# Squares summed by a stationary block of ones in column quarters, z tiles made half a group ahead, y kept in the place of X, and the rope tables made inside the first feed-forward stage

## The chip, the cores and the metric

One Trainium2 chip, of which the kernel uses 1 core. The metric is the device time of one execution in microseconds (us). The kernel before the change took 1360.01 us (median of 3 runs, 1358.56 to 1360.58). One more execution was recorded by the hardware profiler: it took 1358.62 us, of which the profile's span covers 1356.9.

Engines are named as in the profile: PE is TensorE (matrix multiplication), PEld its loading of weights, DVE is VectorE, ACT is ScalarE, POOL is GpSimd, SP is SyncE, which here issues the DMAs. Banks are the eight PSUM tiles `ps` of 128 x 512 that PE writes.

## What is computed

A decoder trunk of 512 tokens by 1024 channels in float32: one Mamba-2 (SSD) layer, a feed-forward layer, one multi-head latent attention layer (MLA), a second feed-forward layer, each with a post-normalisation. The change lies in the SSD layer and in the rotary tables that MLA reads:

```python
zxbcdt = x @ in_proj                       # z, x, B, C and dt side by side
xbc = silu(causal_depthwise_conv(xbc, conv_w, conv_b))
dt = softplus(dt + dt_bias);  A = -exp(A_log)
# 8 groups of 4 heads of 64 channels, state 128; 4 chunks of 128 tokens:
cum = cumsum(dt * A);  decay = exp(where(causal, cum[t] - cum[s], -inf))
w = einsum(C, B) * decay * dt
y = einsum(w, x) + einsum(C, state) * exp(cum)
state = state * exp(cum[-1]) + einsum(exp(cum[-1] - cum) * dt, x, B)
y = (y + D * x) * silu(z)                  # 256 channels a group
y = y * rsqrt(mean(y * y over the group) + 1e-5) * norm_g
h = y @ out_proj                           # then the norm, feed-forward, MLA, feed-forward
cos, sin = cos(positions * inv_freq), sin(positions * inv_freq)   # 512 x 32
```

## The kernel before, in words

Channels lie on partitions and tokens along the free axis. Every large product is taken in three passes over a high and a low part: weights come by DMA on SP into one of three buffers `wst`, ACT casts them to `wh` (L60), DVE takes the rest `wl` (L61), and six such pairs are kept, split up to four items ahead (five in the first feed-forward). `WStream` hands them out in the order of a list of items. `bulk` (matmuls at L123) turns one item of 128 output channels into one bank: 24 matmuls with 512 moving columns.

**The SSD stage** (0 to about 433 us of the span) goes through 8 groups. For each group the program writes four conv tiles, B, C, X0 and X1 (`a_tile`: a bulk, then ACT scales the bank at L438, DVE adds three taps at L440, ACT takes a tanh at L442, DVE finishes at L443), then two z tiles (`z_tiles`: a bulk, then a tanh on ACT at L506 and L507 on DVE). Group 0 has its z from the front of the kernel, where PE computes it beside dt.

The scan of a group is a chain of six steps:

- s0 loads the group's cumulated decays into W by DMA.
- s1 multiplies C with B (L525) and transposes B (L528); DVE masks the result (L530), ACT makes CE (L537), which POOL multiplies by C (L538), and turns W into the decay by 16 relus (L542) and one exponential over 2048 columns (L543).
- s2 transposes X on PE (L550); DVE multiplies W by the masked product (L554) and makes xdt (L559) and wx (L561).
- s3 multiplies wx with B to new states (L568; ACT and DVE chain them at L570 to L575) and W with xdt (L579).
- s4 adds the states' part (L587), then makes y: L593 adds D * x, L594 multiplies by z, ACT squares (L595) and scales by the norm's weight into `yT` (L598), DVE takes its low part (L599), and L602 adds the two squares to `sq` (128 channels by 512 tokens).
- s5 sums `sq` over its 128 partitions: four matmuls at L608 with `sq` as the stationary operand and one moving column of ones; DVE (L610) and POOL (L611) make `rstd`.

The steps stand in a list with due times (`later`). After each tile a clock made by hand advances by its expected time (`tick`), and a step is written into the program once its condition holds, with lags between the steps from `LAG`. Between the tiles of most groups stand blocks of the output projection (`out_block`, matmuls at L129 to L131, added to `h` by DVE at L149). On PE, ACT, DVE and POOL a scheduler then sets the final order from the program's dependences, with its own estimates; each engine runs its own instructions strictly in the order so fixed. On SP the order is that of the program.

The buffers matter: `one` holds a single buffer for each name, so W, CE, bk, xdt, wx (which shares its place with `sq`), y and the pair of z tiles `zs` are each there once; conv tiles have eight buffers. The residual x goes into `h` by one DMA in group 1 (L726), and ACT scales it in group 2 (L729).

**The first feed-forward** (`ffn`, from about 433 us) goes through its 22 hidden tiles with two products each, in two rounds. Between SSD and `ffn` the program builds the rotary tables (`rope_tables`): two small DMAs on SP, some ten small DVE instructions, one sine on ACT.

The order of the work after that point is the same in both kernels on every engine.

Of the kernel before, what the change touches and what calls it, by code (L numbers as in the profile page):

```python
# [9 lines left out]
F32 = mybir.dt.float32  # L10
# [8 lines left out]
P = 128  # L19
# [227 lines left out]
    nc.vector.tensor_tensor(gt[:, 1, :], av, gt[:, 0, :], op=ALU.subtract)  # L247


def ffn(k, ws, base, cwp, gb, la=2, out=None):  # L250

    nc, tc = k.nc, k.tc
    with ExitStack() as c:
# [7 lines left out]
        for r in range(2):  # L261
            gts = []
            def finish(ci, bg, bv):
                gt = pools["gt"].tile([P, 2, SEQ], F32R, name="gt")
                conv3_silu_gate(k, pools, bg, bv, cw, ci, gt)
                gts.append(gt)
# [18 lines left out]
            for ci in range(c0, r * 11 + 11):  # L285
                bg, bv = k.bank(), k.bank()
                ws.ahead(n + 1)
                for b, i in ((bg, n), (bv, n + 1)):
                    w = [x.rearrange("p (k m) -> p k m", k=KT) for x in ws.get(i)]
                    k.mm_a(b, w, k.ht, slice(0, 512))  # L290
                    ws.retire(i)
                n += 2
                ws.ahead(n)
                finish(ci, bg, bv)
            for hf in range(2):
                sl = slice(hf * 512, (hf + 1) * 512)
                final = r == 1 and hf == 1
# [63 lines left out]
def ssd_items(xbc, zdt, zw, ow):  # L361

    it = []
    for a, b in ZDT:
        it.append((zdt[:, a:b, :], (b - a) * ZW))
    for g in range(NG):
        for t in (16 + g, 24 + g, 2 * g, 2 * g + 1):
            it.append((xbc[t], 1024))
        for j in range(2 if g else 0):
            it.append((zw[2 * g + j], 1024))  # L370
        if g in OUT_AT:
            it += [(ow[r * P:(r + 1) * P, :], 1024) for r in (2 * OUT_AT[g], 2 * OUT_AT[g] + 1)]
    it += [(ow[r * P:(r + 1) * P, :], 1024) for r in range(2 * NG - 6, 2 * NG)]
    return it


def ssd(k, ws, base, xT, x, cwp, hv, ngp, gb):
    nc, tc = k.nc, k.tc
    with ExitStack() as cx:
# [129 lines left out]
        def chain(g):  # L509
# [73 lines left out]
            def s4():  # L583
                yb = S["yb"]
                for c in range(1, NT):
                    for t, e, h in heads:
                        nc.tensor.matmul(yb[t][e * HD:(e + 1) * HD, c * P:(c + 1) * P], S["st"][c - 1][:, h * HD:(h + 1) * HD],  # L587
                                         S["CE"][:, h, (c - 1) * P:c * P], start=False, stop=True, skip_group_check=True)
                q = [thp.tile([P, SEQ], F32, name="th") for _ in range(2)]
                y = one.tile([P, 2, SEQ], F32, name="y")  # L590
                for t in range(2):
                    j = 2 * g + t
                    nc.vector.scalar_tensor_tensor(y[:, t], S["X"][t], ng[:, 1, j:j + 1], yb[t], op0=ALU.mult, op1=ALU.add)  # L593
                    nc.vector.scalar_tensor_tensor(y[:, t], y[:, t], 0.5, S["z"][:, t], op0=ALU.mult, op1=ALU.mult)  # L594
                    nc.scalar.activation(q[t], y[:, t], AF.Square)  # L595
                    yt = ytp.tile([P, 2, SEQ], F32R, name="yT")
                    sc = ng[:, 0, j:j + 1]
                    nc.scalar.activation(yt[:, 0, :], y[:, t], AF.Copy, scale=sc)  # L598
                    nc.vector.scalar_tensor_tensor(yt[:, 1, :], y[:, t], sc, yt[:, 0, :], op0=ALU.mult, op1=ALU.subtract)  # L599
                    S.setdefault("yT", []).append(yt)  # L600
                S["sq"] = one.tile([P, SEQ], F32, name="sq", tag="wx")
                nc.vector.tensor_tensor(S["sq"], q[0], q[1], op=ALU.add)  # L602

            def s5():

                b = k.bank()
                for c in range(NT):
                    nc.tensor.matmul(b[:, c:c + 1], S["sq"][:, c * P:(c + 1) * P], ones[:, 0:1], start=True, stop=True)  # L608
# [4 lines left out]
            S.update(s0=s0, s1=s1, s2=s2, s3=s3, s4=s4, s5=s5)  # L613

        T = [0.0]
        todo = []
# [20 lines left out]
            G[g]["s0"]()  # L637
            ran["w", g] = T[0]

        def z_tiles(g):  # L640
            S = G[g]
            S["z"] = one.tile([P, 2, SEQ], F32, name="zs")
            for t in range(2):
                z_gate(S["z"][:, t], bulk())
                tick(5.2)

        def z_turn():

            zs = G[0]["z"] = one.tile([P, 2, SEQ], F32, name="zs")
            for t in range(2):  # L650
                b = k.bank()
                for c in range(NT):
                    nc.tensor.transpose(b[:, c * P:(c + 1) * P], D["z0"][:, c, t * P:(t + 1) * P], k.ident)
                nc.scalar.copy(zs[:, t], b)
# [65 lines left out]
        for g in range(NG):  # L720
            S = G[g]
            if g == 0:
                z_dt()
            S["B"] = a_tile(16 + g)
            if g == 1:
                nc.sync.dma_start(k.h, x.rearrange("(i p) d -> p i d", p=P))  # L726
            if g == 2:
                for i in range(NT):
                    nc.scalar.mul(k.h[:, i, :], k.h[:, i, :], ALPHA)  # L729
# [448 lines left out]
```

## Time and profile before

| | value |
|---|---|
| runs | 1360.01 us median, 1358.56 to 1360.58 |
| profiled execution | 1358.62 us, span 1356.9 |
| granted TensorE clock, mean | 0.998 |
| PE busy | 1341.7 us (99%) |
| DVE busy | 885.6 us (65%) |
| ACT busy | 585.6 us (43%) |
| POOL busy | 71.5 us (5%) |
| SSD stage on PE | 0 to 433.1 us |

How to read the views that follow. The *page* gives busy times by engine and the shares of the chain of waits, which is followed back from the last instruction. *Waits* has, for each engine and line, what ended its idle time: total us, number of times, the longest. The *timeline* has one row for each burst of instructions: start and length in us, engine, line and operation, output and inputs with their shapes, how many instructions, and in brackets the idle time ahead of it with what ended it. The *chain of waits* lists start, length and piece. Line numbers are those of the kernel before; in the changed kernel the steps from s1 to s4 stand one line further down.

### The profile page before, as it was taken

The numbers are of one execution on the slowest core, as the hardware profiler recorded it, in microseconds if no ns is written. First come the engines' busy times: TensorE is split into PE (matmuls) and PEld (weight loads), VectorE is DVE, ScalarE is ACT, GpSimd is POOL, SyncE is SP. The second block draws the span as 40 slices with busy tenths as digits, with TensorE's granted clock in tenths as the row PEclk, the third lists the DMA queues.
The fourth block names the chain that finished last, engine by engine and source line by source line (L and its number), as shares of the span: only waits on it lengthen the run. The fifth ranks groups of instructions, "written<-read, shape, count | busy, mean of one in ns | idle before, by whom it ended". The sixth has DMA issues, their size and how long they took to land.

```text
span 1356.9 us, 17211 instructions
## 1 busy us (share of the span) xinstructions
PE 1341.7 (99%) x6819; PEld 1127.2 (83%) x6819; DVE 885.6 (65%) x1355; ACT 585.6 (43%) x927; POOL 71.5 (5%) x73
## 2 busy tenths in 40 slices
PE   9999999999999999999999999999999999999997
PEld 8878888888888888888888889888898888888886
DVE  7888778778788765425565366998576553465534
ACT  5765536526523544323443134665254431344421
POOL 0111101001102000000000021000100000000001
PEclk9999999999999999999999999999999999999999
DMA  7432332323232433232322222211052322323211
GB/s 240 179 118 95 108 120 82 109 100 103 96 106 64 143 102 100 85 101 95 106 95 85 85 88 65 92 48 63 31 189 93 98 96 89 106 94 102 91 55 63
DMA packets 44433, 135.14 MB, mean 100 GB/s; under 512 B 4768, under 2 KB 5792, under 8 KB 42816
## 3 DMA queue, kind: packets, MB, share of 16 engines
q1 hardware_dynamic: 44352, 134.04, 30.2%
q8 instruction: 53, 0.87, 0.3%
q14 instruction: 28, 0.23, 0.1%
HBM read 131.86 MB, written 2.16 MB: 99 GB/s over the span
## 4 chain that ended last, share of the span: by engine, by line
PE 91%; DVE 5%; DMA 2%; ACT 1%; issue 1%; POOL 0%; SPq 0%; POOLq 0%; DVEq 0%; ACTq 0%
PE ps L123 54%; PE ps L129 9%; PE ps L130 9%; PE ps L131 9%; PE ps L996 2%; PE ps L579 1%; PE ps L1031 1%; DVE wl L61 1%; PE ps L587 1%; PE ps L568 1%; DMA wst<-in_hw_dram 1%; PE ps L1018 1%; PE ps L680 1%; PE ps L205 1%; PE ps L525 0%
## 5 line engine op out<-in xcount | busy, mean ns | idle before, releaser
L123 PE MATMUL ps<-ht,wh 128*128 128x512 f32 (+1 forms) x2272 | 520.2, 379 | 0.8 <-ACT ht L208 0.8
L123 PEld LDWEIGHTS ps<-ht,wh 128*128 128x128 f32 x2272 | 408.4, 188 | 79.8 <-issue 1.2
L61 DVE TENSOR_TENSOR wl<-wst,wh 128x1024 fp32r<-128x1024 f32 (+3 forms) x226 | 273.9, 1217 | 155.9 <-ACT wh L60 155.6
L60 ACT CAST wh<-wst 128x1024 fp32r<-128x1024 f32 (+3 forms) x226 | 228.0, 1014 | 225.7 <-PE ps L131 171.0
L123 PE MATMUL ps<-ht,wl 128*128 128x512 f32 (+1 forms) x1136 | 267.2, 377 | 0.0
L123 PEld LDWEIGHTS ps<-ht,wl 128*128 128x128 f32 x1136 | 205.8, 188 | 39.5
L130 PE MATMUL ps<-wl,gt 128*128 128x512 f32 (+1 forms) x363 | 140.5, 387 | 0.0
L129 PE MATMUL ps<-wh,gt 128*128 128x512 f32 (+1 forms) x363 | 140.1, 386 | 0.0
L131 PE MATMUL ps<-wh,gt 128*128 128x512 f32 (+1 forms) x363 | 138.6, 382 | 0.0
L240 DVE SCALAR_TENSOR_TENSOR acc<-ps,cw,acc 128x511 f32<-128x511 f32 x88 | 65.5, 747 | 99.5 <-ACT acc L239 99.5
L440 DVE SCALAR_TENSOR_TENSOR cv<-ps,cw,cv 128x511 f32<-128x511 f32 (+2 forms) x96 | 71.5, 746 | 28.6 <-ACT cv L438 27.9
L239 ACT ACTIVATE acc<-ps,cw 128x512 f32<-128x512 f32 x88 | 68.4, 778 | 40.2 <-PE ps L123 40.2
L129 PEld LDWEIGHTS ps<-wh,gt 128*128 128x128 f32 x363 | 68.1, 188 | 14.9
L131 PEld LDWEIGHTS ps<-wh,gt 128*128 128x128 f32 x363 | 68.1, 188 | 14.4
L130 PEld LDWEIGHTS ps<-wl,gt 128*128 128x128 f32 x363 | 68.3, 188 | 12.8
L246 ACT CAST gt<-acc 128x512 fp32r<-128x512 f32 x44 | 27.3, 621 | 98.9 <-DVE acc L245 98.9
L149 DVE SCALAR_TENSOR_TENSOR h<-h,ps 128x512 f32<-128x512 f32 x47 | 31.2, 684 | 56.7 <-PE ps L131 56.7
L241 DVE SCALAR_TENSOR_TENSOR acc<-ps,cw,acc 128x510 f32<-128x510 f32 x88 | 65.7, 748 | 2.8
L244 ACT ACTIVATE acc<-acc 128x512 f32<-128x512 f32 x44 | 27.8, 632 | 87.0 <-DVE acc L241 86.9
L149 DVE SCALAR_TENSOR_TENSOR h<-ps,rstd,h 128x512 f32<-128x512 f32 x64 | 46.3, 749 | 21.9 <-PE ps L131 21.3
L159 POOL TENSOR_SCALAR lnst<-lnst 128x1 f32<-128x1 f32 x15 | 11.9, 796 | 870.7 <-ACT lnjunk L158 870.7
L129 PE MATMUL ps<-wh,yT 128*128 128x512 f32 x128 | 51.8, 405 | 0.0
(227 smaller groups left out, 1549.8 us busy)
## 6 DMA issues: line engine op xcount, KB each, us to landing
wst<-in_up_dram SPq DMA_DIRECT2D x88, 512.0 KB, 3.4
wst<-in_down_dram SPq DMA_DIRECT2D x40, 512.0 KB, 3.6
wst<-in_xbc_dram SPq DMA_DIRECT2D x32, 512.0 KB, 3.7
W<-cumd SPq DMA_DIRECT2D x8, 1024.0 KB, 4.6
wst<-in_sow_dram SPq DMA_DIRECT2D x16, 512.0 KB, 3.6
wst<-in_zw_dram SPq DMA_DIRECT2D x14, 512.0 KB, 3.5
lngb<-in_gb_dram SPq DMA_DIRECT2D x4, 1024.0 KB, 6.0
wst<-in_aow_dram SPq DMA_DIRECT2D x8, 512.0 KB, 3.4
```

Source lines behind the costliest of these rows:

```text
L60: nc.scalar.copy(h[:, :f], s[:, :f])
L61: nc.vector.tensor_tensor(l[:, :f], s[:, :f], h[:, :f], op=ALU.subtract)
L123: nc.tensor.matmul(out, w[:, k, :], xts[k][:, x, ts], start=first and p == 0 and k == 0, stop=last and p == 2 and k == nk - 1, skip_group_ ...
L129: nc.tensor.matmul(out, xt[:, 0, tsl], wh, start=start, stop=False, skip_group_check=True)
L130: nc.tensor.matmul(out, xt[:, 0, tsl], wl, start=False, stop=False, skip_group_check=True)
L131: nc.tensor.matmul(out, xt[:, 1, tsl], wh, start=False, stop=stop, skip_group_check=True)
L149: self.nc.vector.scalar_tensor_tensor(hs, a, scale, b, op0=ALU.mult, op1=ALU.add, **kw)
L239: nc.scalar.activation(a, b, AF.Identity, bias=cw[:, ch, 3:4], scale=cw[:, ch, 2:3])
L240: nc.vector.scalar_tensor_tensor(a[:, 1:], b[:, :SEQ - 1], cw[:, ch, 1:2], a[:, 1:], op0=ALU.mult, op1=ALU.add)
L241: nc.vector.scalar_tensor_tensor(a[:, 2:], b[:, :SEQ - 2], cw[:, ch, 0:1], a[:, 2:], op0=ALU.mult, op1=ALU.add)
L244: nc.scalar.activation(ag, ag, AF.Silu)
L440: nc.vector.scalar_tensor_tensor(t[:, d:], b[:, :SEQ - d], cw[:, ch, 3 - d:4 - d], t[:, d:], op0=ALU.mult, op1=ALU.add)
```

## The change

It has four parts.

1. **The sum of squares.** Where s5 had `sq` as the stationary operand and one column of ones moving, it now has 32 columns of ones stationary and a chunk of 128 tokens of `sq` moving. Each of the four matmuls writes 32 equal rows, chunk c to the rows 32c to 32c + 31 of the bank, so each uses its own quarter of PE's columns. ACT copies the 128 x 128 result to `ss`. A new step s6, due 2.6 us of the hand-made clock later, transposes `ss` on PE, and DVE reads every 32nd column of that.
2. **z tiles.** z has three buffers of one tile each instead of one pair. At the end of group g the program makes the second z tile of group g and the first one of group g + 1; so group 0 ends with one z tile (it had none) and group 7 with one (it had two). The list of weight items follows. Group 0's first z, made at the front, sits in the place of CE rather than of y.
3. **y in place of X.** y has no tile of its own: L593 to L599 write over X.
4. **Rope tables.** They are built within the first feed-forward, after the hidden tiles of the first round, instead of between the two stages.

```diff
-def ffn(k, ws, base, cwp, gb, la=2, out=None):
+def ffn(k, ws, base, cwp, gb, la=2, out=None, mid=None):
...
                 finish(ci, bg, bv)
+            if mid and not r:
+                mid()
             for hf in range(2):
...
-        for j in range(2 if g else 0):
-            it.append((zw[2 * g + j], 1024))
+        it += [(zw[j], 1024) for j in (2 * g + 1, 2 * g + 2) if 2 < j + 1 <= 2 * NG]
...
-                y = one.tile([P, 2, SEQ], F32, name="y")
                 for t in range(2):
                     j = 2 * g + t
-                    nc.vector.scalar_tensor_tensor(y[:, t], S["X"][t], ng[:, 1, j:j + 1], yb[t], op0=ALU.mult, op1=ALU.add)
-                    nc.vector.scalar_tensor_tensor(y[:, t], y[:, t], 0.5, S["z"][:, t], op0=ALU.mult, op1=ALU.mult)
+                    y = S["X"][t]
+                    nc.vector.scalar_tensor_tensor(y, y, ng[:, 1, j:j + 1], yb[t], op0=ALU.mult, op1=ALU.add)
+                    nc.vector.scalar_tensor_tensor(y, y, 0.5, S["z"][t], op0=ALU.mult, op1=ALU.mult)
...
                 b = k.bank()
                 for c in range(NT):
-                    nc.tensor.matmul(b[:, c:c + 1], S["sq"][:, c * P:(c + 1) * P], ones[:, 0:1], start=True, stop=True)
+                    nc.tensor.matmul(b[32 * c:32 * c + 32, :P], ones[:, :32], S["sq"][:, c * P:(c + 1) * P], start=True, stop=True)
+                S["ss"] = one.tile([P, P], F32, name="ss")
+                nc.scalar.copy(S["ss"], b[:, :P])
+
+            def s6():
+
+                b = k.bank()
+                nc.tensor.transpose(b[:, :P], S["ss"], k.ident)
                 rs = rstd[:, g]
-                nc.vector.tensor_scalar(rs, b[:, :NT], 1.0 / GC, LN_EPS, op0=ALU.mult, op1=ALU.add)
+                nc.vector.tensor_scalar(rs, b[:, 0:P:32], 1.0 / GC, LN_EPS, op0=ALU.mult, op1=ALU.add)
                 nc.gpsimd.tensor_tensor(rs, rs, k.mhalf.broadcast_to([P, NT]), op=ALU.pow)
...
-        def z_tiles(g):
-            S = G[g]
-            S["z"] = one.tile([P, 2, SEQ], F32, name="zs")
-            for t in range(2):
-                z_gate(S["z"][:, t], bulk())
-                tick(5.2)
+        def z_tile(g, t):
+            z = one.tile([P, SEQ], F32, name="zs", bufs=3)
+            G[g].setdefault("z", []).append(z)
+            z_gate(z, bulk())
+            tick(5.2)
...
-            zs = D["z0"] = one.tile([P, NT, GC], F32, name="y")
+            zs = D["z0"] = one.tile([P, NT, GC], F32, name="z0", tag="CE")
...
             later((5, g), S["s5"], 0.0, [((4, g), LAG[4])])
+            later((6, g), S["s6"], 0.0, [((5, g), 2.6)])
             tick(5.2)
             if g:
-                z_tiles(g)
+                z_tile(g, 1)
+            if g + 1 < NG:
+                z_tile(g + 1, 0)
...
-        rope_tables(k, d['pos'], d['freq'])
-        n = ffn(k, ws, n, d['cw3'][0], d['gb'][1], la=5)
+        n = ffn(k, ws, n, d['cw3'][0], d['gb'][1], la=5, mid=lambda: rope_tables(k, d['pos'], d['freq']))
```

How this moves instructions is shown at three places. First PE in group 1, from its s2 (the transposes of X) to its s3 (`wx,bk`), where a run of 24 `ht` matmuls is one bulk. Before, with the sums of group 0 in front of s3:

```order
L550 MATMUL ps<-ident,cv 128x128 x8
L123 MATMUL ps<-ht,wh 128x512 x8
L123 MATMUL ps<-ht,wl 128x512 x8
L123 MATMUL ps<-ht,wh 128x512 x16
L123 MATMUL ps<-ht,wl 128x512 x8
L123 MATMUL ps<-ht,wh 128x512 x8
L608 MATMUL ps<-ones,sq 128x1 x4
L568 MATMUL ps<-wx,bk 128x256 x3
```

The changed kernel, from the same transposes on:

```order
L551 MATMUL ps<-ident,cv 128x128 x8
L123 MATMUL ps<-ht,wh 128x512 x8
L123 MATMUL ps<-ht,wl 128x512 x8
L123 MATMUL ps<-ht,wh 128x512 x8
L609 MATMUL ps<-sq,ones 32x128 x4
L123 MATMUL ps<-ht,wh 128x512 x8
L123 MATMUL ps<-ht,wl 128x512 x8
L123 MATMUL ps<-ht,wh 128x512 x8
L616 MATMUL ps<-ident,ss 128x128
L569 MATMUL ps<-wx,bk 128x256 x3
```

Between s2 and s3 there are two bulks in both (tiles B and C of group 2); the sums stand between them now, and their transpose stands in front of s3. Ahead of these rows the two z tiles have moved too: before, z(1,1) alone stood between s1 and s2 of group 1, and now z(1,1) stands ahead of s1 and z(2,0) between s1 and s2.

The second place is DVE at the same point, from the decay product `W` to `wx`, which s3 waits for (`cv` is tile B of group 2, `wl` the low part of a weight item, `zs` a z tile). Before:

```order
L554 TENSOR_TENSOR W<-W,cbm 128x2048
L61 TENSOR_TENSOR wl<-wst,wh 128x1024
L440 SCALAR_TENSOR_TENSOR cv<-ps,cw_108,cv 128x511
L440 SCALAR_TENSOR_TENSOR cv<-ps,cw_108,cv 128x510
L61 TENSOR_TENSOR wl<-wst,wh 128x1024
L440 SCALAR_TENSOR_TENSOR cv<-ps,cw_108,cv 128x509
L443 SCALAR_TENSOR_TENSOR cv<-th,cv 128x512
L561 TENSOR_TENSOR wx<-ps,wend 128x512
L561 TENSOR_TENSOR wx<-ps,wend 128x256
```

The changed kernel:

```order
L555 TENSOR_TENSOR W<-W,cbm 128x2048
L508 SCALAR_TENSOR_TENSOR zs<-zs,ps 128x512
L560 TENSOR_TENSOR xdt<-ps,dt 128x512 x2
L61 TENSOR_TENSOR wl<-wst,wh 128x1024
L562 TENSOR_TENSOR wx<-ps,wend 128x512
L562 TENSOR_TENSOR wx<-ps,wend 128x256
L441 SCALAR_TENSOR_TENSOR cv<-ps,cw_108,cv 128x511
```

Between W and the first half of wx stood two weight items and the whole finish of tile B; now there are one z product, the two xdt (which stood ahead of W before) and one weight item, and tile B's taps come behind wx.

The third place is PE's tail of the stage, in the output projection (`yT`), at the sums of group 7. Before:

```order
L130 MATMUL ps<-wl,yT 128x512
L131 MATMUL ps<-wh,yT 128x512
L608 MATMUL ps<-ones,sq 128x1 x4
L129 MATMUL ps<-wh,yT 128x512
L130 MATMUL ps<-wl,yT 128x512
```

The changed kernel:

```order
L130 MATMUL ps<-wl,yT 128x512
L131 MATMUL ps<-wh,yT 128x512
L609 MATMUL ps<-sq,ones 32x128 x4
L616 MATMUL ps<-ident,ss 128x128
L129 MATMUL ps<-wh,yT 128x512
L130 MATMUL ps<-wl,yT 128x512
```

Here nothing of PE's stands between the sums and the transpose of their copy.

More of the change, by code (lines that the diff above doesn't have):

```diff
@@ L589, in s4 @@
                 q = [thp.tile([P, SEQ], F32, name="th") for _ in range(2)]
-                y = one.tile([P, 2, SEQ], F32, name="y")
                 for t in range(2):
                     j = 2 * g + t
-                    nc.vector.scalar_tensor_tensor(y[:, t], S["X"][t], ng[:, 1, j:j + 1], yb[t], op0=ALU.mult, op1=ALU.add)
-                    nc.vector.scalar_tensor_tensor(y[:, t], y[:, t], 0.5, S["z"][:, t], op0=ALU.mult, op1=ALU.mult)
-                    nc.scalar.activation(q[t], y[:, t], AF.Square)
+                    y = S["X"][t]
+                    nc.vector.scalar_tensor_tensor(y, y, ng[:, 1, j:j + 1], yb[t], op0=ALU.mult, op1=ALU.add)
+                    nc.vector.scalar_tensor_tensor(y, y, 0.5, S["z"][t], op0=ALU.mult, op1=ALU.mult)
+                    nc.scalar.activation(q[t], y, AF.Square)
                     yt = ytp.tile([P, 2, SEQ], F32R, name="yT")
                     sc = ng[:, 0, j:j + 1]
-                    nc.scalar.activation(yt[:, 0, :], y[:, t], AF.Copy, scale=sc)
-                    nc.vector.scalar_tensor_tensor(yt[:, 1, :], y[:, t], sc, yt[:, 0, :], op0=ALU.mult, op1=ALU.subtract)
+                    nc.scalar.activation(yt[:, 0, :], y, AF.Copy, scale=sc)
+                    nc.vector.scalar_tensor_tensor(yt[:, 1, :], y, sc, yt[:, 0, :], op0=ALU.mult, op1=ALU.subtract)
                     S.setdefault("yT", []).append(yt)
@@ L607, in s5 @@
                 for c in range(NT):
[L608 removed]
+                    nc.tensor.matmul(b[32 * c:32 * c + 32, :P], ones[:, :32], S["sq"][:, c * P:(c + 1) * P], start=True, stop=True)
[4 more added lines that the diff above has]
+                nc.tensor.transpose(b[:, :P], S["ss"], k.ident)
                 rs = rstd[:, g]
[L610 removed]
+                nc.vector.tensor_scalar(rs, b[:, 0:P:32], 1.0 / GC, LN_EPS, op0=ALU.mult, op1=ALU.add)
                 nc.gpsimd.tensor_tensor(rs, rs, k.mhalf.broadcast_to([P, NT]), op=ALU.pow)
[L613 removed]
+            S.update(s0=s0, s1=s1, s2=s2, s3=s3, s4=s4, s5=s5, s6=s6)
         T = [0.0]
@@ L638, in start_w @@
             ran["w", g] = T[0]
-        def z_tiles(g):
-            S = G[g]
-            S["z"] = one.tile([P, 2, SEQ], F32, name="zs")
-            for t in range(2):
-                z_gate(S["z"][:, t], bulk())
-                tick(5.2)
+        def z_tile(g, t):
[3 more added lines that the diff above has]
+            tick(5.2)
         def z_turn():
-            zs = G[0]["z"] = one.tile([P, 2, SEQ], F32, name="zs")
+            zs = G[0]["z"] = [one.tile([P, SEQ], F32, name="zs", bufs=3) for _ in range(2)]
             for t in range(2):
@@ L653, in z_turn @@
                     nc.tensor.transpose(b[:, c * P:(c + 1) * P], D["z0"][:, c, t * P:(t + 1) * P], k.ident)
-                nc.scalar.copy(zs[:, t], b)
+                nc.scalar.copy(zs[t], b)
         def z_dt():
-            zs = D["z0"] = one.tile([P, NT, GC], F32, name="y")
+            zs = D["z0"] = one.tile([P, NT, GC], F32, name="z0", tag="CE")
             bs = [k.bank() for _ in range(NT)]
```

## The prediction

> **What bounds the kernel now.** I read the page first, for which engine carries the span:
>
> ```profile
> PE 1341.7 (99%) x6819; PEld 1127.2 (83%) x6819; DVE 885.6 (65%) x1355; ACT 585.6 (43%) x927; POOL 71.5 (5%) x73
> PE 91%; DVE 5%; DMA 2%; ACT 1%; issue 1%; POOL 0%; SPq 0%; POOLq 0%; DVEq 0%; ACTq 0%
> ```
>
> PE is busy for 99% of the span and is 91% of the chain of waits, at a granted clock of 0.998. So the time can change in two ways only: PE's own work, or the 15 us in which PE stands still. The waits of PE say where those are:
>
> ```profile
> PE ps L568 <- DVE wx L561: 3.0, 1, 3.0
> PE ps L205 <- DVE h L166: 0.9, 1, 0.9
> PE ps L123 <- ACT ht L208: 0.8, 1, 0.8
> ```
>
> One wait stands out: s3 waits once for wx, 3.0 us. It is in group 1; PE's timeline there:
>
> ```profile
> 76.90 1.53 PE L587 MATMUL ps<-CE,st 128*64 128x128 f32 x24
> 78.36 1.16 PE L525 MATMUL ps<-cv 128*128 128x128 f32 x8
> ...
> 96.94 0.95 PE L608 MATMUL ps<-ones,sq 128*128 128x1 f32 x8
> 100.86 1.56 PE L568 MATMUL ps<-wx,bk 128*128 128x256 f32 x6 [2.98 <-DVE wx L561]
> ```
>
> Why wx came late is read from DVE, POOL and ACT in the same stretch:
>
> ```profile
> 78.26 1.40 DVE L593 SCALAR_TENSOR_TENSOR y<-cv,ng,ps 128x512 f32<-128x512 f32 x2 [3.12 <-PE ps L587]
> 79.59 4.60 DVE L594 SCALAR_TENSOR_TENSOR y<-y,zs 128x512 f32<-128x512 f32 x2
> ...
> 85.84 0.68 DVE L507 SCALAR_TENSOR_TENSOR zs<-zs,ps 128x512 f32<-128x512 f32 x1
> ...
> 88.37 1.28 DVE L559 TENSOR_TENSOR xdt<-ps,dt 128x512 f32<-128x512 f32 x2
> ...
> 92.10 2.29 DVE L554 TENSOR_TENSOR W<-W,cbm 128x2048 f32<-128x2048 f32 x1 [1.12 <-ACT W L543]
> 94.31 1.22 DVE L61 TENSOR_TENSOR wl<-wst,wh 128x1024 fp32r<-128x1024 f32 x1
> 95.44 1.53 DVE L440 SCALAR_TENSOR_TENSOR cv<-ps,cw,cv 128x511 f32<-128x511 f32 x2
> 96.89 1.21 DVE L61 TENSOR_TENSOR wl<-wst,wh 128x1024 fp32r<-128x1024 f32 x1
> ...
> 99.52 0.69 DVE L443 SCALAR_TENSOR_TENSOR cv<-th,cv 128x512 f32<-128x512 f32 x1 [0.76 <-ACT th L442]
> 100.13 1.01 DVE L561 TENSOR_TENSOR wx<-ps,wend 128x512 f32<-128x512 f32 x2
> ```
> ```profile
> 80.10 3.54 POOL L538 TENSOR_TENSOR CE<-CE,cv 128x1536 f32<-128x1536 f32 x1 [23.11 <-ACT CE L537]
> ```
> ```profile
> 90.17 1.90 ACT L543 ACTIVATE W<-W 128x2048 f32<-128x2048 f32 x1
> ```
>
> Two instructions at L594 took 4.60 us, where two of the same kind and shape at L593 took 1.40: the 3.2 us between them lie within the 3.54 us in which POOL ran, and DVE hardly moved. That pushed ACT's exponential to 90.17, and behind L554 wx then queued after two weight items and all of tile B, 8.0 us from 92.10 to 100.13. wx asks only for the transposes of X, so it is its place in the queue that made it late.
>
> **The stall of group 1.** PE's order in the change puts one more bulk ahead of s3(1): after s4(0) at 76.90 to 78.36 come z(1,1), s1, z(2,0), s2, tile B, the sums, tile C, the transpose of the sums. The prices are pieces of the chain in later groups:
>
> ```profile
> 151.05 1.46 PE ps L587 x24
> 152.51 16.59 PE ps L123 x72
> 169.10 0.79 PE ps L608 x8
> 169.88 5.55 PE ps L123 x24
> 176.66 5.46 PE ps L123 x24
> 182.12 0.87 PE ps L550 x8
> ```
>
> Before, s1 is the stretch from 78.36 to the start of the next bulk at about 79.6, 1.2 us. A bulk is 5.46 us, or 5.55 behind a block in plain f32, and 5.68 behind a block like s4 (16.59 is three bulks and 0.21). So s3(1) is due at 78.36 + 5.68 + 1.2 + 5.55 + 0.87 + 5.55 + 0.6 + 5.46 + 0.2 = 103.5. There wx is needed; before it was done at 101.1. Even with wx as late as before, PE would not wait. On DVE it should come earlier: behind the exponential now stand 2.29 (W), 0.68 (z), 1.28 (xdt) and 1.22 (one weight item), 5.2 us as the rows follow each other (each starts some 0.08 before the last one's end), where there were 8.0. With the exponential at its old time that is 97.3 to 98.3; the z tile in between is ready (its bulk ends at 90.8). s1 itself stands 5.7 us later, but the relus and the exponential need only the decays, and the mask at L530 is 0.68 us of DVE. I take 99 for wx; if POOL blocks DVE once more for its whole 3.54 us, 102.5. Both are below 103.5. Removed: from L608's start to L568's 3.92 us, less 0.79 of L608, **3.1 us**.
>
> What is late next? First the residual. Its DMA is moved behind one more weight load on SP:
>
> ```profile
> h<-in_x_dram SPq DMA_DIRECT2D x1, 2048.0 KB, 10.1
> 47.17 0.43 SPq L726 DMA_DIRECT2D h<-in_x_dram  x1
> ```
> ```profile
> 62.52 1.04 ACT L729 ACTIVATE h<-h 128x1024 f32<-128x1024 f32 x1
> ```
> ```profile
> 74.73 0.42 DVE L575 TENSOR_TENSOR st<-st,ps 128x256 f32<-128x256 f32 x1
> ```
>
> A load more is one bulk more on SP, so the issue falls at about 53 and, 10.1 us on, ACT can scale at 63.3 instead of 62.52. ACT's queue behind it, up to the states of group 0, slips by about 0.8 to 1.2 us: the last state at 76.3 where it was 75.15. s4(0) uses it in its last third, from about 77.9. Margin 1.6 us: no cost taken, 1 us if it is wrong.
>
> Second, group 7, which now has one bulk less ahead of s3:
>
> ```profile
> 371.34 0.89 PE ps L525 x8
> 388.13 1.29 PE ps L568 x6
> ```
> ```profile
> 381.73 0.41 DVE L561 TENSOR_TENSOR wx<-ps,wend 128x256 f32<-128x256 f32 x1
> ```
>
> From s1 to s3 PE took 16.8 us and wx was done after 10.8. In the new order 48 projection matmuls stand there, at 5.46 / 24 each, 10.9, with s1 1.2, s2 0.87 and the sums and their transpose 0.8: 13.8. So wx has 3 us to spare, less about 0.8 if the new copy and a z product come ahead of it. No cost.
>
> **The sums of squares.** Eight groups, each a block of 8 passes (an f32 matmul is counted twice). The old block is 0.79, and the bulk behind it is 5.55 instead of 5.46: 0.88. A pass with 128 moving columns is 0.87 / 8 = 0.109 (L550). How four quarters go is not in the trace; the nearest row on the fast side is L587, with two halves of the columns: 24 passes in 1.46 us, 0.061 each, so two go at once: 12 pairs of 0.109 are 1.31, 0.15 goes on entry, and 0.21 on leaving (16.59 above). On the slow side stands dt's part, whose 32-column operands lie in one quarter:
>
> ```profile
> 42.52 0.99 PE ps L479 x8
> ```
>
> There 8 passes are 0.99, one after the other. If the four quarters go at once, the new block is 2 x 0.109 + 0.15 + 0.21 = 0.58, and the transpose 0.22: 0.80 against 0.88. If two by two, 1.02; if one by one, 1.45. I take the first, as L587 shows tiles in different columns going together, and only the same columns waiting for each other. [...] Seven groups: -0.08 each, or nothing if the transpose costs 0.09 behind it as L608 did; -0.3 in all. In the last group the transpose stands right behind the sums, and PE waits for ACT's copy:
>
> ```profile
> 44.30 0.25 ACT L490 COPY cum<-ps 128x128 f32<-128x128 f32 x1
> ```
>
> At least 0.25, at most the 0.8 of the wait at L208, which is also PE to ACT to PE: I take 0.6. That block is 0.58 + 0.22 + 0.6, less the 0.21 on leaving, which lies within the wait: 1.19 against 0.88, +0.3. **Together 0.0**, between -0.6 and +0.6. The copies on ACT, 8 x 0.25, lie in its 57% of idle time, DVE's strided read of 4 columns replaces one of 4 columns, and rstd is used only a projection block later.
>
> **z tiles and y over X.** The number of bulks is the same. y over X lengthens the life of two of the eight conv buffers by the few us of L594 to L599; their next owners are tiles of two groups later, no cost. Three z buffers let a tile be written before s4 has read the last pair; ACT's tanh no longer waits for L594. Nothing of it is on PE's path beyond the stall already counted.
>
> **Rope tables.** At the seam PE waits 0.9 us for DVE's norm (L205 <- L166), with rope's first cast just ahead of that on DVE:
>
> ```profile
> 440.34 0.17 DVE L814 CAST posf<-posi 128x4 f32<-128x4 int32 x1
> ...
> 442.89 1.41 DVE L166 SCALAR_TENSOR_TENSOR h<-h,lnst,lngb 128x512 f32<-128x512 f32 x2
> ```
> ```profile
> 569.51 1.23 DVE L61 TENSOR_TENSOR wl<-wst,wh 128x1024 fp32r<-128x1024 f32 x1 [4.27 <-ACT wh L60]
> ```
>
> The cast can have cost at most 0.17; I take -0.1. In its new place, the projection at the end of round one, DVE idles 4.27 us per weight item, more than its 12 small instructions need, 2 us at the cast's 0.17; its two small DMAs go onto SP between weight loads, and the sine onto an ACT that is idle for more than half of the span. If the cover were gone, those 2 us would be the cost.
>
> **Sum.** -3.1 + 0.0 - 0.1 = -3.2 us on the profiled 1358.62, so 1355.4 there; that execution lies 1.4 below the median of the runs, and on the median's scale it is 1360.01 - 3.2 = **1356.8**.
>
> **Rivals.**
> - *Two quarters at a time*: 8 x 0.22 = +1.8, so 1358.6. For it: L587 shows two and no row more.
> - *One by one*: 8 x 0.65 = +5.2, net +2.0, 1362.0. For it only L479, which uses one quarter.
> [...]
> - *The stall moves*: wx slips behind 103.5 (POOL's block, and a weight item that comes late), the last state of group 0 misses by 1 us, or a z tile's tanh ahead of ACT's exponential holds another group's W. Then 0.5 to 3 us come back: 1357.3 to 1359.8. At its end the change does nothing that shows: the reordering trades one wait for an equal one.
> - *The seam also gains*: with rope gone, DVE's norm moves up and the 0.9 at L205 goes: 1355.9.
>
> **How the numbers follow.** Forecast 57%, two by two 13%, one by one 9%, stall moves 11%, drained quarters 7%, the seam 3%. The range takes the forecast with the bounds of the sums (and run to run 1 us either way), two by two and the moved stall: 1354.6 to 1360.4, about 83%. A measurement of this kernel can tell 0.2%, 2.7 us, from no change; 1357.3 is that line. Of the forecast's 57, some 50 lie below it, with the seam's 3 and a little of the moved stall 55 for faster; drained quarters and the upper edge of one by one give 8 for slower; 37 for the same.
>
> **What would show it.** Right: no wait of PE for wx above 0.3 us; s3(1) starting near 103.5 with wx done 2 us or more before; DVE's L594 pairs without 4.6 us; L609 with 8 passes starting within 0.3 us in the trace and its block about 0.58; one wait of PE at L616, in group 7, about 0.6; the feed-forward starting about 3.2 us earlier. Wrong: L609 blocks of 0.9 or more, a wait at L569 in another group, at L588 for st, or a span gained or lost behind 450 us, where the order is the same.

## The result, and the profile after

The changed kernel takes **1354.27 us** (median of 6 runs, 1353.71 to 1355.31), the kernel before beside it 1359.83 us (6 runs, 1358.56 to 1360.80): 5.6 us less, a ratio of 0.9959 with a 95% interval of 0.9949 to 0.9970. The forecast was 3.2 us less, and the measured time lies 0.3 us below its range. The profiled executions are 4.55 us apart (1358.62 and 1354.07, spans 1356.9 and 1352.3). So there are two things to explain: what made up the 4.55, and why the medians differ by one microsecond more.

The page of the changed kernel has the same bound as before, PE:

```profile
PE 1340.1 (99%) x6827; PEld 1121.3 (83%) x6827; DVE 881.8 (65%) x1355; ACT 585.7 (43%) x934; POOL 70.9 (5%) x73
PE 94%; DVE 3%; ACT 1%; DMA 1%; issue 1%; POOL 0%; SPq 0%; POOLq 0%; DVEq 0%; ACTq 0%
```

PE's waits of the changed kernel (engine, line, what it waited for: total, times, longest):

```profile
PE ps L123 <- ACT ht L208: 1.1, 1, 1.1
PE ps L405 <- DVE warm L99: 1.1, 1, 1.1
PE ps L551 <- DVE cv L444: 0.7, 1, 0.7
PE ps L616 <- ACT ss L611: 0.4, 1, 0.4
PE ps L205 <- DVE h L166: 0.4, 1, 0.4
```

The 3.0 us for wx are gone. Two small waits are new: 0.7 at L551 (s2) and 0.4 at L616 (the transpose of the sums). PE's timeline in group 1, at the place where the stall was, and DVE's:

```profile
96.71 0.43 PE L609 MATMUL ps<-sq,ones 128*32 128x128 f32 x8
97.06 2.12 PE L123 MATMUL ps<-ht,wh 128*128 128x512 f32 x8
...
102.65 0.27 PE L616 MATMUL ps<-ident,ss 128*128 128x128 f32 x1
102.76 1.46 PE L569 MATMUL ps<-wx,bk 128*128 128x256 f32 x6
```
```profile
95.98 1.22 DVE L61 TENSOR_TENSOR wl<-wst,wh 128x1024 fp32r<-128x1024 f32 x1
97.20 1.02 DVE L562 TENSOR_TENSOR wx<-ps,wend 128x512 f32<-128x512 f32 x2
```

s3(1) starts at 102.76, foreseen for 103.5, and wx is done at 98.2, foreseen for 99. L569 has no wait in brackets. The sums and their transpose, as pieces of the chain of waits in a steady group:

```profile
222.51 0.35 PE ps L609 x8
222.86 5.68 PE ps L123 x24
228.54 0.11 PE ps L616
```

0.35 for the block and 0.22 on the bulk behind it (5.68 against 5.46) make 0.57, foreseen as 0.58. The transpose is one pass of 0.11 and not two. From one run of three bulks to the next, a steady group took 51.99 us before and takes 51.83 now; first the kernel before, then the changed one:

```profile
204.50 16.59 PE ps L123 x72
...
256.49 16.59 PE ps L123 x72
```
```profile
205.92 16.59 PE ps L123 x72
...
257.75 16.59 PE ps L123 x72
```

Added up on PE's starts: stall and its restart -3.2; seven blocks of sums at -0.16, -1.1; the last block, with its wait, +0.2; the wait at L551 with what stands around it, +1.0; the seam to the feed-forward -0.2. That is -3.3. The remaining -0.4 at the front and -0.8 in the attention are waits for DMAs and for what DVE makes behind them. The experiments show whether they belong to the change.

### The profile page after: what moved, and what is told of

Its sections match the earlier page's. It is cut to its first block, busy times and chain, and to the rows that moved or that the text cites. A ratio compares the mean times of both kernels' runs of the same rounds, so it can differ in the third digit from the quotient of the medians.

```text
span 1352.3 us, 17236 instructions
## 1 busy us (share of the span) xinstructions
PE 1340.1 (99%) x6827; PEld 1121.3 (83%) x6827; DVE 881.8 (65%) x1355; ACT 585.7 (43%) x934; POOL 70.9 (5%) x73
## 4 chain that ended last, share of the span: by engine, by line
PE 94%; DVE 3%; ACT 1%; DMA 1%; issue 1%; POOL 0%; SPq 0%; POOLq 0%; DVEq 0%; ACTq 0%
PE ps L123 55%; PE ps L129 10%; PE ps L130 10%; PE ps L131 10%; PE ps L1006 2%; PE ps L580 1%; PE ps L1041 1%; PE ps L569 1%; PE ps L588 1%; PE ps L1028 1%; PE ps L687 1%; DVE wl L61 1%; PE ps L205 1%; PE ps L551 1%; PE ps L526 0%
```

## The experiments

All are compared with the kernel before on the same chip: 1359.6 to 1359.8 us in the median of 12 to 18 runs there. Line numbers differ by 1 or 2 between the kernels; operations and tiles tell which line it is.

**1. Sums in quarters and y over X, without the moved z tiles and rope tables.** The list of items, `z_tiles` and the call of `rope_tables` are those of before; the rest is as in the change. Of the edit this is the call:

```diff
...
             if g:
-                z_tile(g, 1)
-            if g + 1 < NG:
-                z_tile(g + 1, 0)
+                z_tiles(g)
...
```

> The sums in column quarters and y over X, with the z tiles in pairs at the end of their own group and the rope tables between the stages, both as in the kernel before. My theory (order of the z tiles removes the stall, the sums save a little by themselves): PE's wait for wx in group 1 stays and is 3.0 to 3.5 us, since the shorter sums ahead of it only lengthen it; no wait of L551's kind in group 7, since both z tiles are ahead of it; the groups 3 to 6 are 0.16 us shorter each; the time is 0.5 to 1.2 us under the kernel before. Rival (y's own buffer or the old form of the sums held up DVE and so made the stall): the wait for wx is under 1 us, and the time is 3 us or more under the kernel before.

Measured: 1358.43 us (11 runs), ratio 0.9994 (0.9985 to 1.0003): the interval holds no change at all, so the 1.2 us between the medians are not shown. The stall is there, with no wait at s2 of group 7, and steady groups are 51.82 us apart. But the rows behind the stall held a surprise:

```profile
96.55 0.43 PE L610 MATMUL ps<-sq,ones 128*32 128x128 f32 x8
100.38 2.93 PE L570 MATMUL ps<-wx,bk 128*128 128x256 f32 x6 [3.41 <-DVE wx L563]
103.24 3.56 PE L581 MATMUL ps<-W,xdt 128*64 128x128 f32 x32
```

The six matmuls of s3 take 2.93 us instead of 1.56, the next 32 take 3.56 instead of 1.97. The view by windows gives the granted clock (each engine's busy time and instructions, then PEclk as the third number from the end, DMA share, GB/s):

```profile
97.00:100.50 3.50, 0.12 (x1) 0.12 (x1) 2.75 (x5) 2.13 (x4) 0.00 (x0) 0.89 0.74 242
100.50:104.00 3.50, 3.50 (x14) 2.49 (x16) 3.50 (x6) 0.64 (x2) 0.00 (x0) 0.50 0.03 12
104.00:107.00 3.00, 3.00 (x29) 2.80 (x26) 1.84 (x5) 0.63 (x1) 0.00 (x0) 0.58 0.00 0
107.00:110.00 3.00, 3.00 (x14) 2.44 (x14) 0.00 (x0) 0.00 (x0) 0.00 (x0) 1.00 0.74 300
```

By the trace's records of the granted clock it is at half from 99.71 to 106.53 us, 6.8 us, of which the first 0.7 still belong to the stall. From s3's start to the next bulk PE took 6.34 us, where the kernel before took 3.39 in its first profile. That costs 3 us more, which no wait shows, as PE counts as busy.

**2. The changed kernel with the old sums.** L609 and its step are those of before, and step s6 is left out.

```diff
-                    nc.tensor.matmul(b[32 * c:32 * c + 32, :P], ones[:, :32], S["sq"][:, c * P:(c + 1) * P], start=True, stop=True)
+                    nc.tensor.matmul(b[:, c:c + 1], S["sq"][:, c * P:(c + 1) * P], ones[:, 0:1], start=True, stop=True)
```

> The changed kernel with the old sums of one moving column. My theory: the wait for wx in group 1 is gone all the same, the steady groups have their old length (52.0 us from one group to the next), the wait for tile X1 in group 7 is there but shorter than 1 us, as the longer sums stand ahead of it, and no wait for the copy in the last group. The time is 2.8 to 3.6 us under the kernel before, some 1 us above the changed kernel. Rival (the sums carry most of the gain): 1.5 us or less under the kernel before.

Measured: 1354.81 us, 0.9967 (0.9956 to 0.9978), so 4.8 us under the kernel before. Missed: I had 2.8 to 3.6. Its steady groups are 52.0 us apart and the wait at L551 is 0.2, as expected. By the profiles the sums are worth 0.85 us up to the seam. What the forecast lacked is the price of the stall.

**3. The rope tables between the stages again**, in the changed kernel:

```diff
-        n = ffn(k, ws, n, d['cw3'][0], d['gb'][1], la=5, mid=lambda: rope_tables(k, d['pos'], d['freq']))
+        rope_tables(k, d['pos'], d['freq'])
+        n = ffn(k, ws, n, d['cw3'][0], d['gb'][1], la=5)
```

> The changed kernel with the rope tables between the two stages again. My theory: PE starts the first feed-forward's second half 0.1 to 0.3 us later against its transposes, nothing else changes: the time is 4.4 to 5.6 us under the kernel before. Rival (rope's place also moves DVE's and the DMAs' timing in the attention, where the changed kernel's profile shows 0.8 us less waiting): the waits of 0.4 us each of the attention come back, and the time is 3.5 to 4.5 us under the kernel before.

Measured: 1354.41 us, 0.9965 (0.9952 to 0.9977): the time of the change. At the seam PE waits 0.42 us at L205, where the changed kernel waits 0.36. The place of the rope tables is worth nothing that can be measured, in either direction. This kernel differs from that of experiment 1 in the z tiles alone, and PE no longer waits for wx: of the change's four parts it is the move of the z tiles that removes the stall.

**4. Other work behind the last sums.** Twelve matmuls of the projection are put between the last sums and their transpose.

```diff
-        while todo:
+        while len(todo) > 1:
+            tick(1.0)
+        out_part(NG - 2, 2)
+        while todo:
             tick(1.0)
...
-            if i >= 2:
+            if i >= 3:
                 out_part(NG - 2, i, retire=i == NT - 1)
```

> The changed kernel with twelve projection matmuls of group 6 put between the last group's sums and the transpose of their copy. My theory: PE's wait of 0.4 us at L616 goes, and with it 0.5 us; 4.9 to 6.1 us under the kernel before, 0.3 to 0.6 us less from the end of the last state's matmuls to the end of the stage's projection. Rival (the later rstd holds up DVE's adds and through them PE's banks or the norm at the seam): the wait comes back at the seam, no gain or a loss of up to 1 us.

Measured: 1354.79 us, 0.9969 (0.9957 to 0.9980), no gain over the change. The wait at L616 is gone, and the wait at the seam has grown from 0.4:

```profile
PE ps L205 <- DVE h L166: 1.1, 1, 1.1
```

The rival holds: PE waits at the seam for DVE's norm, and what PE gains shortly ahead of it is given back there.

**5. A place of its own for sq.** This tests the reason that the prediction gave for the late wx. `sq` and `wx` share one buffer, so wx of group 1 may only be written after PE has read sq of group 0. The kernel is that of before, with y over X (to make room; group 0's first z then sits in the place of CE, as in the change) and

```diff
-                S["sq"] = one.tile([P, SEQ], F32, name="sq", tag="wx")
+                S["sq"] = one.tile([P, SEQ], F32, name="sq")
```

PE's order is that of the kernel before, and on DVE wx moves up.

> The kernel before with y over X and, in the room that this frees, a place of its own for sq, which otherwise shares one with wx. Sums, z tiles and rope tables are as before, and PE's order is the same row for row. My theory (wx of group 1 was late because it may be written only when PE has read sq of group 0 at L608, which stands right before s3 on PE): wx is now written before that, PE's wait of 3.0 us at s3(1) goes, and with it the lower clock that follows it in some executions: 3.1 us by the profile, 3.5 to 4.5 us by the median. Rival (the place in DVE's queue behind POOL's block and the weight items made wx late, whatever the buffer): a wait of 1 us or more stays at s3(1), and the gain is under 2 us.

Measured: **1354.68 us** (8 runs), 0.9967 (0.9956 to 0.9977): 4.9 us under the kernel before, without the new sums, the z order or the rope move, and a little more than the 3.5 to 4.5 expected. DVE's and PE's rows:

```profile
79.71 4.60 DVE L596 SCALAR_TENSOR_TENSOR cv<-cv,zs 128x512 f32<-128x512 f32 x2
...
89.09 0.68 DVE L563 TENSOR_TENSOR wx<-ps,wend 128x512 f32<-128x512 f32 x1
...
91.03 0.41 DVE L563 TENSOR_TENSOR wx<-ps,wend 128x256 f32<-128x256 f32 x1
92.23 2.29 DVE L556 TENSOR_TENSOR W<-W,cbm 128x2048 f32<-128x2048 f32 x1 [0.79 <-ACT W L545]
```
```profile
97.07 0.95 PE L610 MATMUL ps<-ones,sq 128*128 128x1 f32 x8
97.88 1.54 PE L570 MATMUL ps<-wx,bk 128*128 128x256 f32 x6
```

The 4.60 us beside POOL's run are still there, the exponential is as late as before (92.23 against 92.10 for W), and yet wx is done at 91.4, six microseconds before s3 asks for it. The rival, my own reason, falls. The late place of wx in DVE's queue was real, but it followed from the shared buffer: without it the scheduler put both halves of wx ahead of W.

**6. The same kernel without that one edit**: y over X alone, sq still in the place of wx. It is the control of 5.

> The kernel before with y over X alone: sq keeps its place in common with wx, all else is as before. My theory (the shared place of sq and wx made the stall, and y over X by itself does nothing): the wait for wx at s3(1) is 2.9 to 3.1 us as before, and the time is within 0.1% of the kernel before, in its spread too (1357 to 1362). Rival (y's own buffer held up the chain): the wait falls by 1 us or more.

Measured: 1359.38 us (10 runs), 0.9997 (0.9988 to 1.0007). The stall is back to 2.98 us, and in the profiled execution with half clock behind it:

```profile
100.88 2.92 PE L570 MATMUL ps<-wx,bk 128*128 128x256 f32 x6 [2.98 <-DVE wx L563]
103.74 2.05 PE L581 MATMUL ps<-W,xdt 128*64 128x128 f32 x32
```

Here the half clock lasts 3.4 us, from 100.54 (by windows the granted clock is 0.97 from 97.00 to 100.80 us, 0.51 to 104.00 and 1.00 to 107.00), and only s3's first matmuls take about twice their time, 2.92 us for six instead of 1.56.

**7. The kernel before once more**, unchanged, for a second profile:

> The kernel before once more, for a second profile of its stall. My theory (the stall of 3 us is long enough that the granted clock drops to half behind it in some executions and not in others): the wait for wx is again 2.9 to 3.4 us, and if the execution takes over 1360 us, the granted clock of the 6 us behind the wait is below 1, the matmuls of s3 taking twice their time. Rival (the executions above 1360 differ elsewhere, in the DMAs of the front or the attention): full clock behind the stall, and the excess stands in waits at L680, L996 or L1018.

Measured: 1361.24 us in this execution, with a mean granted clock of 0.996. The stall is the same to the hundredth, and what follows is not:

```profile
101.05 2.93 PE L568 MATMUL ps<-wx,bk 128*128 128x256 f32 x6 [2.98 <-DVE wx L561]
103.91 3.58 PE L579 MATMUL ps<-W,xdt 128*64 128x128 f32 x32
```
```profile
97.00:100.50 3.50, 1.07 (x10) 0.95 (x8) 2.74 (x5) 1.46 (x3) 0.00 (x0) 0.99 0.70 212
100.50:104.00 3.50, 2.95 (x8) 1.94 (x10) 2.70 (x7) 1.14 (x2) 1.04 (x1) 0.50 0.18 74
104.00:107.00 3.00, 3.00 (x30) 3.00 (x32) 3.00 (x5) 0.63 (x1) 0.00 (x0) 0.50 0.00 0
```

The first profile of the same kernel, on which the prediction rests, had full clock there:

```profile
100.80:104.00 3.20, 3.13 (x36) 2.70 (x38) 3.20 (x9) 0.99 (x3) 1.04 (x1) 1.00 0.03 13
104.00:107.00 3.00, 3.00 (x18) 2.35 (x15) 2.40 (x4) 0.30 (x1) 0.00 (x0) 1.00 0.56 177
```

So one and the same stall of 2.98 us costs 3.1 us in one execution and 6.1 in another. The whole stage says the same: from the start of s4(0) to the transposes that open the feed-forward (L205), PE took 351.15 us in kernel 5, which has no stall, and 354.29, 355.72 and 357.29 in the three profiles with it (the first of the kernel before, kernel 6, and this one). That is 3.1, 4.6 and 6.1 us, with no half clock behind the stall, 3.41 us of it, and 6.83. Among the first 18 runs of the kernel before beside these experiments, the two with a mean clock of 0.998 took 1357.0 and 1360.1 us, the five at 0.996 took 1360.5 to 1362.4, and the eleven at 0.997 lie between, at 1358.5 to 1360.2. The profiled execution with 0.998 was one of the rarer, faster ones.

**8. The sums in two halves**, 64 columns of ones and two transposes, in the changed kernel (the copy, the transposes and the strided read follow):

```diff
-                    nc.tensor.matmul(b[32 * c:32 * c + 32, :P], ones[:, :32], S["sq"][:, c * P:(c + 1) * P], start=True, stop=True)
+                    nc.tensor.matmul(b[64 * (c % 2):64 * (c % 2) + 64, c // 2 * P:(c // 2 + 1) * P], ones[:, :64], S["sq"][:, c * P:(c + 1) * P], start=True, stop=True)
...
```

> The changed kernel with the sums in two column halves (64 columns of ones, two chunks a half, two transposes) instead of four quarters. My theory (tiles in different columns go at once, the same columns wait): the eight passes start in four pairs 0.11 us apart, the block takes 0.22 us more and the second transpose 0.11: a steady group is 0.3 us longer than in the changed kernel, 2.6 us in all. Rival (four quarters had not gone at once, or PE's cost is mostly the entry and exit): under 0.1 us more per group.

**9. All four in one quarter**, with four small transposes:

```diff
-                    nc.tensor.matmul(b[32 * c:32 * c + 32, :P], ones[:, :32], S["sq"][:, c * P:(c + 1) * P], start=True, stop=True)
+                    nc.tensor.matmul(b[:32, c * P:(c + 1) * P], ones[:, :32], S["sq"][:, c * P:(c + 1) * P], start=True, stop=True)
...
```

> The changed kernel with all four sums in one quarter of the columns (32 columns of ones, output rows 0 to 31, four small transposes). My theory: the eight passes go one after the other, 0.11 us each, the block takes 0.65 us more and the three further transposes 0.2 to 0.35: a steady group is 0.85 to 1.0 us longer than in the changed kernel, 7 to 8 us in all. Rival (passes with few columns overlap even in one quarter): 0.3 us or less per group.

Measured, one execution each: 1359.90 and 1363.54 us. The price is read from the block itself, in the chain of waits of 8 and of 9:

```profile
224.54 0.59 PE ps L609 x8
225.13 5.71 PE ps L123 x24
230.84 0.22 PE ps L617 x2
```
```profile
226.42 0.99 PE ps L609 x8
227.41 5.66 PE ps L123 x24
233.08 0.36 PE ps L617 x4
```

Eight passes take 0.35 us in four quarters, 0.59 in two halves and 0.99 in one quarter. Steady groups are 51.83, 52.19 and 52.86 us apart, so halves cost 0.36 us more a group and one quarter 1.03, each a little above what was expected. By these three times tiles in different columns go at once, and the same columns wait for each other. The totals are 3 and 1 us longer than eight such blocks explain; 1.1 us of 8's stands in two waits for E in the attention, and single executions tell no more.

**10. s2 of group 7 later**, in the changed kernel:

```diff
-            later((2, g), S["s2"], T[0] + LAG[1], [((1, g), 0.0)])
+            later((2, g), S["s2"], T[0] + LAG[1] + (2.6 if g == NG - 1 else 0.0), [((1, g), 0.0)])
```

> The changed kernel with s2 of group 7 due 2.6 us later on the hand-made clock, so that twelve projection matmuls more stand ahead of its transposes. My theory (the wait of 0.7 us at L551 comes from the bulk that group 7 has lost: the transposes are due before DVE has finished tile X1): the wait goes, PE gains 0.9 to 1.0 us up to the end of the stage's projection. Of the whole time 0.5 to 1.0 us stay, unless the seam takes them as it took the 0.5 us of the last sums. Rival (wx and s3 slip by as much): the wait comes back at s3(7), no gain.

Measured: 1354.46 us, 0.9960 (0.9948 to 0.9973); the changed kernel beside it 1354.52. The wait at L551 is gone and 0.9 us are gained up to the seam, but nothing of that is left in the time: at the seam L205 waits 1.1 us instead of 0.4. DVE's order shows a reason, which was not tried by itself: two weight items stand ahead of the last adds to h, where the changed kernel has one.

```profile
431.00 2.35 DVE L61 TENSOR_TENSOR wl<-wst,wh 128x1024 fp32r<-128x1024 f32 x2
433.27 0.75 DVE L149 SCALAR_TENSOR_TENSOR h<-ps,rstd,h 128x512 f32<-128x512 f32 x1
```

**11. Own place for sq, y over X and the quarters**, with z and rope as before: kernel 5 with the sums of the change.

> The kernel before with y over X, a place of its own for sq and the sums in column quarters; z tiles and rope tables as before. My theory: neither the wait for wx in group 1 (sq's own place) nor the one for X1 in group 7 (no bulk lost), and the steady groups 0.16 us shorter: 0.7 to 1.2 us under the changed kernel, 5.0 to 6.5 under the kernel before. Rival (the seam between the stages hides what PE gains ahead of it): the time of the changed kernel, 4.5 to 5.2 us under the kernel before.

Measured: **1353.41 us** (5 runs, 1352.86 to 1354.01), 0.9953 (0.9940 to 0.9965): 6.4 us under the kernel before. All five runs lie below all five of the changed kernel beside it. PE's waits:

```profile
PE ps L123 <- ACT ht L208: 1.1, 1, 1.1
PE ps L406 <- DVE warm L99: 1.1, 1, 1.1
PE ps L205 <- DVE h L166: 0.5, 1, 0.5
PE ps L617 <- ACT ss L612: 0.4, 1, 0.4
PE ps L689 <- ACT wh L60: 0.2, 1, 0.2
```

Neither the wait for wx nor that for the conv tile is there, and this time the seam takes nothing back. It is the fastest version of the study, and it moves no z tile.

**12. The changed kernel once more:**

> The changed kernel once more, on the chip of the other three and for a second profile. My theory: no wait over 1.3 us of PE in the trace and no stretch of lower clock behind 20 us, so its runs lie closer together (1.6 us) than those of the kernel before (4 to 5 us); 4.5 to 5.6 us under it. The waits at the front (L687) and in the attention (L1006, L1028) differ from the first profile by up to 1 us, as they do not belong to the change.

Measured: 1354.52 us (5 runs, 1354.20 to 1355.60), 0.9962 (0.9950 to 0.9975). Its wait at the front (L687) is 0.9 us where the first profile had 0.2, and between 855 and 864 us, in the attention, PE loses 0.3 us again. In the profiles with the rope tables moved or not, with the new sums or the old, these waits come and go. So the 0.4 and 0.8 us of the account above are differences between executions and not an effect of the change that these runs could show.

## Why the prediction was right or wrong, point by point

- **The stall goes.** Right in place and in size on the profiled execution (3.1 us), and PE's new order gave s3(1) the time it was forecast to have.
- **Luck in the sum.** Up to the seam the profiles show -3.1 us where the forecast had -3.1 + 0.0. That is so because two terms were off by nearly the same amount the other way: the sums gave -0.9 instead of 0.0, and group 7 cost 1.0 instead of nothing.
- **Why wx was late.** Wrong. The prediction said "wx asks only for the transposes of X, so it is its place in the queue that made it late", with POOL's run as its origin. wx asks for its buffer too, which sq of the group before still held until L608, the very block in front of s3. Experiments 5 and 6 differ in that line alone: without the shared place the stall is gone, although POOL's 4.60 us and the late exponential stay. In the change the moved z tiles remove it (experiments 1 and 3). Why they do is argued from the order: a bulk now stands between the sums and s3, so that sq is read, and its place free, more than 5 us before s3, and wx starts at 97.20, right behind L609. DVE's weight item ahead of wx ends then too, so the trace does not tell which of the two held it. POOL's block is still there in the change: the products with z take 0.68 us each, not 4.60 for two, but one instruction that makes yT (L600) takes 2.70 us beside POOL's run where the next takes 0.74, and W starts at 91.97 against 92.10.
- **The scale of the sum.** This is the step that put the time outside the range: "on the median's scale it is 1360.01 - 3.2". It took the distance between the profiled execution and the median as noise that stays. It was part of the stall's own price: half clock behind it, in most executions (by their mean clocks, 0.996 or 0.997 in 16 of 18 runs) but not in the profiled one (0.998). By medians the stall was worth 4.9 us against the kernel before (experiment 5) and 4.7 against kernel 6, which differs in the one line but ran on another chip; the forecast had 3.1. With 4.7 the forecast's sum gives 1355.2, inside the range. The 0.9 us from there to 1354.27 no run here explains: the differences at the front and in the attention come and go between executions.
- **The sums.** The four quarters go at once, as forecast, at 0.57 us a block against 0.58: in a steady group the eight passes start in two sets of four, 0.02 us from first to last in each and 0.15 in all. The transpose was taken at 0.22 and is 0.11, since a transpose is one pass (L550 had shown it: 8 rows for 8 transposes); the forecast also allowed for half of the gain only. Seven groups gave -1.1 us instead of -0.3, the last +0.2 as against +0.3.
- **Group 7.** "No cost" was wrong by 1.0 us. The prediction checked that wx would be in time for s3, but not what s2 itself reads. With one bulk less ahead of it, s2 came while tile X1 was still behind W in DVE's queue:

```profile
375.02 2.29 DVE L555 TENSOR_TENSOR W<-W,cbm 128x2048 f32<-128x2048 f32 x1 [0.45 <-ACT W L544]
377.23 0.69 DVE L444 SCALAR_TENSOR_TENSOR cv<-th,cv 128x512 f32<-128x512 f32 x1
```

- **Residual, y over X, rope tables.** Right: no wait at L588 for the states, nothing from y over X (experiment 6), nothing that can be measured from rope (experiment 3).
- **The rivals.** Serial or paired quarters are refuted by the 0.35 us of L609. That a change of quarter drains PE, to which the prediction gave 7%, no run shows: the eight passes over four quarters start within 0.15 us. A stall did move, to another place than the ones named (s2 of group 7).

## What to carry to other kernels

When an operand comes late, look through the buffers as well as the queues: an instruction that shares its place with an older tile waits for the last reader of that tile (wx for the sums' read of sq: 2.98 us of PE's wait in experiment 6, none in experiment 5), and if the reader stands right in front of the waiting matmul, no faster queue helps. When work is taken from between two steps, check each input of the later step. And the price of a PE stall need not be its length, as the one of 2.98 us shows that cost 3.1, 4.6 and 6.1 us in three executions: look at the granted clock behind it in more than one profile, and at the spread of the runs, before setting a sum made on one execution against a median.

## What the runs showed of the hardware

A stretch of 2.98 us without matmuls was followed by full clock in one profile (the first of the kernel before), by 3.41 us of half clock in a second (kernel 6: 1.45 us of loss, 4.84 us from s3's start to the next bulk instead of 3.39) and by 6.83 us in a third (experiment 7: 3 us of loss); one of 3.41 us by 6.83 (experiment 1). In the first profiles of the kernel before and of the changed one the clock records show one stretch of full clock, of 1344.85 us from 6.83 and of 1341.44 us from 6.77: 394 and 393 times 3.413 us. The half clock of 3.41 and 6.83 us is one and two of these steps. In the 3.41 us that ended with the drop (at 100.54, 100.45 and 99.71 us in experiments 6, 7 and 1) PE had stood still for 2.6, 2.4 and 2.7 us. In the profile that kept full clock, steps counted from 6.83 end at 98.99 and 102.40 us, so that the stall fell into two of them, with 1.1 and 1.9 us. The 3.41 us behind the drop held 0.3, 0.6 and 0.7 us without matmuls: after the first the clock was full again, after the other two it stayed at half for as long once more.

So half clock followed where 3.41 us held at least 2.4 us without matmuls, and did not where the stall was split into 1.1 and 1.9. That the place of the stall in these steps decides is the author's reading of four profiles and was not tried by itself. In two of the three with a drop the eight one-column passes of the sums stood ahead of the stall; whether they mattered no run tells, nor from which length on a stall is safe. The changed kernel, with waits of up to 1.1 us, kept full clock from 6.77 us to its last matmul in the first profile, and had a mean clock of 0.999 in the second.

Eight passes of 128 columns took 0.35 us in four column quarters, 0.59 in two halves and 0.99 in one quarter; each form lengthened the bulk behind it by 0.20 to 0.25.
